# RMSNorm with repeated rows: the first tile by one transfer in place of two halves, gamma in eight pieces in place of seven

## The chip, the cores and the metric

The kernel runs on one core of a Trainium2 chip. The metric is the device time of one execution in microseconds (us), as a median over several executions. The profile's span, from the first to the last instruction, is some 1.8 us shorter than the time: 237.9 us against 239.7 before.

## The reference

```python
# x: (8, 512, 2048) float32, gamma: (2048,) float32
x_rep = np.repeat(x, 2, axis=1)
rms = np.sqrt((x_rep ** 2).mean(axis=-1, keepdims=True) + 1e-6)
return ((x_rep / rms) * gamma[None, None, :]).astype(np.float32)   # (8, 1024, 2048)
```

Each row is normalised, multiplied by gamma and written twice. 33.6 MB come in and 67.1 MB go out.

## The kernel before

The 4096 rows are eight tiles of 128 partitions with four rows each. In the code K = 4 is the rows of a partition and R = 2 the repeats. A tile's buffer holds the 64 KB per partition that go out; x lands in its second half. There are three such buffers, so loads 0, 1 and 2 have free buffers at the start, and each later load waits for a store. All loads and stores are issued by the sync engine, in the order of the program.

```python
def load(i, eng, parts=1):
    y = rows.tile([P, K * R, D], f32, name="y")
    step = K // parts
    for k in range(0, K, step):
        at = K * (R - 1) + k
        eng.dma_start(out=y[:, at : at + step, :], in_=x_t[i, :, k : k + step, :])   # L52
    ys.append(y)
# ... store: nc.sync.dma_start, L56; square: ScalarE, L64 and L68; scale: VectorE, L73 and L74;
# ... repeat: a copy, half on ScalarE and half on VectorE, L81
load(0, nc.sync, parts=2)
gamma_b = singles.tile([P, D], f32, name="gamma_b")
cuts = [0, *range(D // 4, D + 1, D // 8)]            # 512 elements, then six times 256
for c0, c1 in zip(cuts, cuts[1:]):
    nc.scalar.dma_start(out=gamma_b[0:1, c0:c1], in_=gamma[c0:c1].partition_broadcast(1))   # L95
nc.gpsimd.partition_broadcast(out_ap=gamma_b[:], in_ap=gamma_b[0:1, :])                     # L96
# ...
load(1, nc.sync)
load(2, nc.sync)
loads_after = {2: (3, 4, 5), 4: (6, 7)}
for i in range(ntiles):
    compute(i)
    store(i, 0, K)
    for j in loads_after.get(i, ()):
        load(j, nc.sync)
```

The program names no semaphores (counters that a transfer raises when it has landed and for which an engine can wait). The framework gives each transfer one, and this turns out to be what the case is about.

## Time and profile before

| | before |
|---|---|
| time, median of the 5 runs beside the changed kernel | 239.5 us (239.32 to 240.03) |
| span of the profile | 237.9 us |
| VectorE, ScalarE busy | 41%, 42% |
| transfers of the sync queue, share of 16 DMA engines | 98.5% |
| mean rate | 423 GB/s |
| load 1 issued | 8.11 us |
| last packet of load 2 ends | 33.0 us |
| store 0 issued | 27.05 us |

How to read it: only the DMA engines are near full, so what counts is whether their stream has holes. Idle time of the compute engines costs nothing as long as the next store is issued before the engines run dry. Load 2's end and store 0's issue are the pair to compare at the start. The table's last two rows show store 0 six microseconds ahead.

### The profile page before, as it was taken

How to read it: one execution, taken by the hardware profiler on the slowest of the kernel's cores; microseconds unless marked ns; L12 is line 12 of the kernel's file. 1: busy time of each engine (PE TensorE's matmuls, PEld its weight loads, DVE VectorE, ACT ScalarE, POOL GpSimd, SP SyncE). 2: the span in 40 equal slices, each digit the busy share in tenths (PEclk: the TensorE clock that was granted, in tenths of full speed). 3: DMA queues.
4: the chain of work that ended last, by engine and by line, in shares of the span. 5: the costliest groups of instructions: out<-in, count | busy, mean ns of one | idle time of the engine just before them, and what ended most of it. 6: DMA issues, size and time to landing. Idle time of an engine off the chain costs nothing.

```text
span 237.9 us, 287 instructions
## 1 busy us (share of the span) xinstructions
DVE 96.5 (41%) x73; ACT 101.0 (42%) x106; POOL 2.5 (1%) x5
## 2 busy tenths in 40 slices
DVE  0049999960000000059999960000199990000000
ACT  2697999900000000099999920000599960000000
POOL 0030000000000000000000000000000000000000
DMA  7999998989899998999998999989998989999994
GB/s 265 436 446 441 441 441 353 530 353 496 386 452 430 397 485 353 441 441 441 441 518 364 464 419 430 452 369 430 435 518 364 518 364 485 397 452 430 408 474 176
DMA packets 2464, 100.69 MB, mean 423 GB/s; under 512 B 279, under 2 KB 285, under 8 KB 286
## 3 DMA queue, kind: packets, MB, share of 16 engines
q1 hardware_dynamic: 2448, 100.66, 98.5%
q14 instruction: 2, 0.02, 0.0%
q10 hardware_dynamic: 14, 0.01, 0.0%
HBM read 33.56 MB, written 67.11 MB: 423 GB/s over the span
## 4 chain that ended last, share of the span: by engine, by line
DMA 58%; ACT 12%; DVE 9%; issue 1%; POOLq 1%; ACTq 1%; SPq 0%
DMA y<-in_x_dram 33%; DMA out_dram<-y 21%; ACT sq L64 8%; DVE y L74 7%; DMA gamma_b<-in_gamma_dram 4%; ACT y L81 3%; DVE y L81 2%; ACT rms L68 1%; POOLq L136 1%; ACTq L95 1%; DVE rstd L73 0%; POOLq L96 0%; SPq L56 0%
## 5 line engine op out<-in xcount | busy, mean ns | idle before, releaser
L64 ACT ACTIVATE sq<-y 128x2048 f32<-128x2048 f32 x32 | 59.7, 1865 | 87.8 <-DMA y<-in_x_dram 87.8
L74 DVE SCALAR_TENSOR_TENSOR y<-y,rstd,gamma_b 128x2048 f32<-128x2048 f32 x32 | 75.3, 2352 | 4.1 <-POOL gamma_b L96 3.0
L73 DVE RECIPROCAL rstd<-rms 128x1 f32<-128x1 f32 x32 | 5.0, 158 | 94.6 <-ACT rms L68 94.3
L81 ACT COPY y<-y 128x4096 f32<-128x4096 f32 x8 | 28.7, 3590 | 1.4 <-DVE y L74 1.4
L81 DVE COPY y<-y 128x4096 f32<-128x4096 f32 x8 | 18.3, 2294 | 0.3
L68 ACT ACTIVATE rms<-ss,eps_t 128x1 f32<-128x1 f32 x32 | 9.4, 295 | 1.0
L64 ACT ACTIVATION_READ_ACCUMULATOR sq<-y 128x1 f32 x32 | 6.0, 187 | 0.0
L64 ACT ACT_TABLE_LOAD x1 | 1.3, 1283 | 3.0 <-issue 3.0
L96 POOL PARTITION_BROADCAST gamma_b<-gamma_b x1 | 2.3, 2294 | 12.2 <-DMA y<-in_x_dram 12.2
L68 ACT ACT_TABLE_LOAD x1 | 1.3, 1283 | 0.0
L98 DVE MEMSET eps_t<- 128x1 f32 x1 | 0.1, 59 | 0.8 <-PEq L125 0.8
L125 POOL MEMSET const-uint8-127<- 128x1 uint8 x1 | 0.1, 102 | 0.0
L125 POOL MEMSET const-bfloat16-1.0<- 128x1 bf16 x1 | 0.1, 101 | 0.0
L125 POOL MEMSET const-float32-0.0<- 128x1 f32 x1 | 0.1, 98 | 0.2 <-issue 0.2
L125 POOL MEMSET const-float32-1.0<- 128x1 f32 x1 | 0.1, 98 | 0.0
## 6 DMA issues: line engine op xcount, KB each, us to landing
y<-in_x_dram SPq DMA_DIRECT2D x7, 4096.0 KB, 14.6
y<-in_x_dram SPq DMA_DIRECT2D x2, 2048.0 KB, 7.4
out_dram<-y SPq DMA_DIRECT2D x8, 24.4
gamma_b<-in_gamma_dram ACTq DMA_DIRECT2D x6, 1.0 KB
gamma_b<-in_gamma_dram ACTq DMA_DIRECT2D x1, 2.0 KB
```

The source lines that it names most:

```text
L64: nc.scalar.activation(out=sq[:], in_=ys[i][:, K * (R - 1) + k, :], func=Act.Square, accum_out=ss[:])
L68: nc.scalar.activation(out=rms[:], in_=ss[:], func=Act.Sqrt, scale=inv_d, bias=eps_t[:])
L73: nc.vector.reciprocal(out=rstd[:], in_=rms[:])
L74: nc.vector.scalar_tensor_tensor(out=ys[i][:, R * k, :], in0=ys[i][:, K * (R - 1) + k, :], scalar=rstd[:], in1=gamma_b[:], op0=Alu.mult, o ...
L81: copy(out=y_r[:, k0:k1, 1, :], in_=y_r[:, k0:k1, 0, :])
L95: nc.scalar.dma_start(out=gamma_b[0:1, c0:c1], in_=gamma[c0:c1].partition_broadcast(1))
L96: nc.gpsimd.partition_broadcast(out_ap=gamma_b[:], in_ap=gamma_b[0:1, :])
L98: nc.vector.memset(eps_t, eps)
L125: nc = _bacc.Bacc("TRN2", target_bir_lowering=False, num_devices=1)
L136: with _tile.TileContext(nc) as tc:
```

## The change

The intent is fewer and longer transfers: the first tile as one of 4 MB, with 32 KB contiguous per partition and not twice 16 KB, and gamma in eight equal pieces.

```diff
-    load(0, nc.sync, parts=2)
+    load(0, nc.sync)
     gamma_b = singles.tile([P, D], f32, name="gamma_b")
-    cuts = [0, *range(D // 4, D + 1, D // 8)]
+    cuts = [*range(0, D + 1, D // 8)]
     for c0, c1 in zip(cuts, cuts[1:]):
```

## The prediction

> **What bounds the kernel now.** I read the page first: the busy tenths and the queue table.
>
> ```profile
> DVE 96.5 (41%) x73; ACT 101.0 (42%) x106; POOL 2.5 (1%) x5
> ...
> DMA  7999998989899998999998999989998989999994
> ...
> q1 hardware_dynamic: 2448, 100.66, 98.5%
> ```
>
> No compute engine is busy half of the time, while the transfers of the sync queue (q1: all loads of x and all stores) keep the sixteen DMA engines busy for 98.5% of the span. The packet records of the trace (start, length, bytes) say the same more sharply: the first packet of x starts at 1.73 us, the last packet of a store ends at 236.77, and no DMA engine rests for more than 0.34 us anywhere between. A 16 KB packet takes 611 ns, a 32 KB one 1213, a 64 KB one 2418. So the span is a constant sum of bytes plus whatever holes there are in this one stream. **A delay counts if and only if it makes a hole in it.** There are two places at the start where a hole could open, and I looked at both: the issues of loads 0 to 2, and the first store.
>
> The waits of the sync engine, then its timeline from 0 to 2, 2 to 3 and 8.3 to 9 us:
>
> ```profile
> SPq L52 <- DMA y<-in_x_dram: 5.7, 1, 5.7
> ...
> SPq L52 <- DMA gamma_b<-in_gamma_dram: 0.9, 1, 0.9
> ```
>
> ```profile
> 0.72 0.38 SPq L52 DMA_DIRECT2D y<-in_x_dram  x1
> ...
> 2.03 0.33 SPq L52 DMA_DIRECT2D y<-in_x_dram  x1
> ...
> 8.11 0.81 SPq L52 DMA_DIRECT2D y<-in_x_dram  x2
> ```
>
> The source has nothing between the four load issues, and their buffers are free, yet the second half waits 0.9 us for a gamma piece and load 1 waits 5.7 us for the first half of tile 0 to land. The records of the transfers name the semaphores, which explains it. Eight semaphores go round among all transfers in scheduled order, and a transfer that takes a used one waits until its former user has landed. The order is: gamma 1 (first), first half (second), gamma 2 to 7 (third to eighth), second half (first again, hence the wait for gamma 1), load 1 (second again, hence the wait for the first half), load 2 (third again, after gamma 2). Today this costs nothing: when load 1 goes out at 8.11, the second half still has until 12.62 to run on the engines.
>
> The second place, in the timeline from 0 to 32 us:
>
> ```profile
> 8.12 1.88 ACT L64 ACTIVATE sq<-y 128x2048 f32<-128x2048 f32 x1 [3.85 <-DMA y<-in_x_dram]
> ...
> 12.60 2.29 POOL L96 PARTITION_BROADCAST gamma_b<-gamma_b  x1 [12.17 <-DMA y<-in_x_dram]
> ...
> 14.92 2.35 DVE L74 SCALAR_TENSOR_TENSOR y<-y,rstd,gamma_b 128x2048 f32<-128x2048 f32 x1 [3.00 <-POOL gamma_b L96]
> ...
> 27.05 0.35 SPq L56 DMA_DIRECT2D out_dram<-y  x1
> ```
>
> The first scaling waits for gamma (its last piece lands at 12.40 by the chain of waits), and store 0 goes out 12.13 us after it. The DMA engines finish load 2 between 32.41 and 33.00. As an issue needs about 1.0 us to reach the engines (0.72 to 1.73 at the start), store 0 may be as late as 31.4: it has 4.4 us in hand.
>
> **What the Trainium skill says.** "DMA: Bandwidth & Descriptors", section "Queues, rings and completion order": each DMA engine goes round between the queue rows at packet granularity. The trace agrees: gamma's small packets start at 5.65, 6.30, 6.91, 7.56 and so on, one for each 611 ns packet of x. The section "Why a DMA increments its semaphore by 16 and not by 1" says that a copy whose slowest dimension has few elements uses few engines; the trace has 14 packets for 7 gamma transfers (data and semaphore), and the spacing shows all of them queueing behind one engine's packets. The section "Latency and other measured facts" gives about 600 ns to the first byte for transfers issued from sync or scalar; the trace has 1.0 us from the start of the issue to the first packet, and I use that. The section "Rules for kernel authors" asks for at least 1 MiB per DMA; both forms (2 MB, 4 MB) satisfy it, so I expect no gain in rate from the larger one, and the packet times above (2 x 611 against 1213 ns) agree.
>
> **The change part by part.**
>
> *Gamma.* One more issue on the scalar queue, 0.27 us, ahead of an engine that waits for x anyway: nothing. Eight pieces and one load are again nine transfers, so the ring of semaphores comes out the same for all that follows. In scheduled order I expect gamma 1, load 0, gamma 2 to 8, load 1, load 2: the eighth piece takes the first semaphore (free since about 2.0), load 1 takes the second one again, and load 2 the third.
>
> *Load 0 whole.* The bytes, the engines and the stream are those of the two halves, and the second half landed at 13.01; sixteen semaphore packets of 9 ns fewer change nothing, so load 0 lands at about 12.95.
>
> *What moves: load 1's wait.* Its semaphore was that of the first half and is now that of the whole load. It therefore goes out at about 12.96 in place of 8.11, when the engines have run dry, having ended their last packets between about 12.1 and 12.6. The hole can be sized by the same start at the beginning of the kernel: from the issue at 0.72 to the last semaphore packet of the first half at 7.70 are 6.98 us, of which 8 packets x 0.607 = 4.86 us are movement. So a start on empty engines costs 2.12 us. Load 1's last engine then ends at 12.96 + 2.12 + 8 x 1.21 = 24.76, against 22.30 now: **2.5 us later**. A cold first transfer may be slower than this one. With landing 0.4, first byte 1.0 and only some 0.4 us of slow first packets, it would be 1.8. I take 2.2. All of it is on the path that sets the end, since the stream has no slack later in which it could be recovered.
>
> *What moves beside it.* Squares start at 12.97 in place of 8.12. From the first square to the first possible scaling are 3.8 us (8.12 to 11.93, the second table load included), so scaling can start at 16.8, not 14.92. Gamma's pieces meet x packets of twice the length, but only eight of them: in the hole after load 0 the engine is theirs, a piece needs some 0.1 us, and the last should land by 13.8. Broadcast ends by 16.3, before the 16.8. Store 0 goes out at 16.8 + 12.1 = 28.9, 1.9 us later, and load 2 now drains 2.2 us later too: its 4.4 us in hand stay. No second hole.
>
> The sum: 239.7 + 2.2 = **241.9 us**, 0.9% slower.
>
> **The rivals.** *First: load 1 is not held, and gamma starves.* If the scheduled order puts load 1 before gamma 8, load 1 gets the semaphore of gamma 1, goes out at about 2 us, and the stream has no hole at 13. Then each of gamma's packets waits for a 32 KB packet. Five packets of x went before the second piece; with 1.21 us each that puts it at some 8.7 in place of 5.65, and about 12 more turns at 1.24 us end at 23.6. Landing and broadcast put the scaling at 26.5 and store 0 at 38.6, so its packets come at 39.6, 6.8 us after the stream drained: 246.5. If the head start is a time and not five packets, it is about 3 us less: 243.4. For it: the alternation is in the trace. Against it: all gamma pieces preceded the second half in the ring of the kernel before, and load 1 stands where that half stood. *Second: nothing happens*, 239.7: the later tile 0 is hidden by the 4.4 us in hand, and load 1 goes out early for a reason that I don't see. The 5.7 us wait speaks against it. *Third: larger packets are faster.* 611 against 1213/2 ns over 8 packet pairs is below 0.1 us.
>
> **Range and chances.** The hole is 1.8 to 2.5 us by the two ways of sizing, runs of before spread over 0.65 us, and a slow restart or a little of the starved gamma could add one: 241.0 to 243.2. Slower by over 2% means over 244.5, which only the first rival reaches in its worse form: 0.05. Faster has no mechanism: 0.01. Within 2%: 0.94.
>
> **What would show it.** Right: sync waits for x about 11.9 us ahead of load 1, its issue stands near 13.0, few bytes move from 12.6 to 14.5, the first square starts near 13.0, gamma's broadcast starts by 14, store 0 goes out near 29, and the distance from store 0's landing to the end is as now. Wrong: load 1 issued by 3 us or at 8; the scaling waiting for the broadcast until after 20; a hole between load 2 and store 0; or a hole at 13 which the end does not show.

## The result

The changed kernel takes 242.18 us (241.99 to 242.49, five runs), against 239.5 us. The ratio is 1.011, with a 95% interval of 1.0097 to 1.0124. Ratios here are the mean time of one kernel's runs over that of the other's runs in the same rounds, so they aren't quite the ratios of the medians. The change is 1.1% slower: a small loss, clear of noise, and within 2%.

The same parts of the page as before, for the changed kernel (busy time, the DMA row of the slices, the sync queue):

```profile
DVE 96.6 (40%) x73; ACT 101.0 (42%) x106; POOL 2.5 (1%) x5
...
DMA  7979998989898989999999999999999898989894
...
q1 hardware_dynamic: 2304, 100.66, 97.7%
```

The compute engines do what they did. The DMA row has a new 7 in its third slice, which is 12 to 18 us. The waits of the sync engine, and its timeline from 13.2 to 20 us:

```profile
SPq L52 <- DMA y<-in_x_dram: 12.1, 1, 12.1
```

```profile
13.25 0.81 SPq L52 DMA_DIRECT2D y<-in_x_dram  x2
```

The wait of 5.7 us for the first half is now one of 12.1 us for the whole of load 0, and loads 1 and 2 go out from 13.25 us. The wait for a gamma piece is gone, together with the transfer that had it. What this does to the stream is in the table of stretches. Each row gives the stretch, its length, the busy time of VectorE, ScalarE and GpSimd with their instructions, the clock, the mean share of the DMA engines, and GB/s. First before, then changed:

```profile
9.50:12.00 2.50, 0.17 (x1) 2.47 (x5) 0.00 (x0) 1.00 0.98 420
12.00:14.50 2.50, 0.00 (x0) 2.47 (x4) 1.91 (x1) 1.00 0.99 426
14.50:17.00 2.50, 2.08 (x1) 2.47 (x4) 0.39 (x1) 1.00 1.03 446
```

```profile
9.50:12.00 2.50, 0.00 (x0) 0.00 (x0) 0.00 (x0) 1.00 0.97 420
12.00:14.50 2.50, 0.00 (x0) 1.25 (x1) 0.92 (x1) 1.00 0.55 146
14.50:17.00 2.50, 0.10 (x1) 2.47 (x5) 1.38 (x1) 1.00 0.71 275
```

Until 12 us the two are equal at 420 GB/s. Then the changed kernel has 146 GB/s where the kernel before has 426, and 275 GB/s against 446 while the stream restarts. (Rates over short stretches are rough, as a packet's length is of the order of the stretch.) The packet records show the hole engine by engine: the last packets of load 0 end between 11.96 and 12.90 us, and the first ones of load 1 start between 14.21 and 14.68, after 1.3 to 2.7 us. Those sixteen first packets then take 1.71 to 2.12 us in place of 1.21.

Tile 0 in the changed kernel's timeline:

```profile
13.25 1.88 ACT L64 ACTIVATE sq<-y 128x2048 f32<-128x2048 f32 x1 [8.57 <-DMA y<-in_x_dram]
...
13.58 2.29 POOL L96 PARTITION_BROADCAST gamma_b<-gamma_b  x1 [13.16 <-DMA gamma_b<-in_gamma_dram]
...
17.38 2.35 DVE L74 SCALAR_TENSOR_TENSOR y<-y,rstd,gamma_b 128x2048 f32<-128x2048 f32 x1 [0.32 <-DVE rstd L73]
...
29.52 0.35 SPq L56 DMA_DIRECT2D out_dram<-y  x1
```

The first scaling now waits for its own row's statistics and no longer for gamma. Store 0 goes out 2.5 us later than before, but load 2's packets end only at 35.7, so the engines never wait for store 0.

The whole difference can be laid out from the packet records, as means over the sixteen DMA engines, relative to the kernel before. "Idle" is time without a packet of the sync queue, "slow packets" is what packets took beyond 609, 1212 and 2418 ns for 16, 32 and 64 KB (reference values at or 1 to 2 ns below the commonest 611, 1213 and 2418), and "lag" is how far the last engine ends after the mean of the engines:

| us, relative to before | idle | slow packets | lag of the last engine | end of the last packet |
|---|---|---|---|---|
| changed kernel | +2.17 | +0.60 | -0.35 | +2.33 |

The three add up to 2.42. The 0.09 that is missing at the end is rounding, a start that is 0.02 us earlier, and the whole tile's packets, which are 0.05 us shorter in sum (8 x 1212 against 16 x 609 ns). The hole and its restart are the loss.

### The profile page after: what moved, and what is told of

It is laid out like the page before. It is cut to its first block, busy times and chain, and to the rows that moved or that the text cites. A ratio compares the mean times of both kernels' runs of the same rounds, so it can differ in the third digit from the quotient of the medians.

```text
span 240.4 us, 286 instructions
## 1 busy us (share of the span) xinstructions
DVE 96.6 (40%) x73; ACT 101.0 (42%) x106; POOL 2.5 (1%) x5
## 4 chain that ended last, share of the span: by engine, by line
DMA 58%; ACT 13%; DVE 10%; issue 1%; DVEq 0%; SPq 0%
DMA y<-in_x_dram 37%; DMA out_dram<-y 21%; ACT sq L64 8%; DVE y L74 8%; ACT y L81 3%; DVE y L81 2%; ACT rms L68 1%; ACT L68 1%; DVE rstd L73 0%; DVEq L74 0%; SPq L56 0%
## 5 line engine op out<-in xcount | busy, mean ns | idle before, releaser
L96 POOL PARTITION_BROADCAST gamma_b<-gamma_b x1 | 2.3, 2295 | 13.2 <-DMA gamma_b<-in_gamma_dram 13.2
```

## The experiments

The theory is the prediction's: a transfer is held (called the hold below) until the one that had its semaphore eight transfers earlier has landed, and in the changed kernel load 1, the tenth, is held by load 0, the second. The issue records in the traces name the semaphores, and each hold below agrees with them. The main rival is that tile 0 is late as a whole, so that everything after it is. The theory says that the *number* of transfers decides who waits for whom, and numbers are easy to change. All edits are shown against the changed kernel. All results were correct.

### One piece of gamma, load 0 whole: the hold taken away

```diff
-    cuts = [*range(0, D + 1, D // 8)]
+    cuts = [0, D]
```

> Load 0 whole as in the change, gamma in one piece of 8 KB, so that loads 1 and 2 take semaphores nobody has used yet. Theory (the hold of load 1 on load 0's semaphore makes the hole): load 1 goes out by 2 us, no hole at 13 us, first square still at about 13, first scaling at about 17, store 0 at about 29, inside its time in hand: 239.5 us, ratio to before 0.998 to 1.002. Rival (tile 0 coming late as a whole is what the end pays for): as slow as the change, about 242.2, ratio 1.011.

240.29 us (239.68 to 241.37, six runs), ratio 1.0025 (1.0006 to 1.0044). The sync engine's timeline:

```profile
0.72 1.62 SPq L52 DMA_DIRECT2D y<-in_x_dram  x3
29.17 0.35 SPq L56 DMA_DIRECT2D out_dram<-y  x1
```

All three loads are issued by 2.34 us without a wait. The first square still starts at 13.13 and store 0 at 29.17, as late as in the changed kernel, and 2 of the 2.6 us are gone. So the lateness of tile 0 is not what the end pays for. The result is a little above the expected 1.002: 0.6 us remain. In its profile there is no idle time more than before; the last DMA engine lags the mean by 1.57 us, against 0.89.

### Two halves, eight pieces: the hold moved to another place

```diff
-    load(0, nc.sync)
+    load(0, nc.sync, parts=2)
```

> Load 0 in two halves as before, gamma in eight pieces as in the change: ten transfers where both kernels have nine, so the second half now takes the semaphore of the first half. Theory: the second half goes out only at about 8.1, when the engines have run dry at 7.3 to 7.7; the same restart cost as in the change, 2.2 to 2.5 us: 241.7 to 242.1 us, ratio 1.009 to 1.011, with the first square still at 8.1. Rival (tile 0 late as a whole): no loss, 239.5. A rival that blames gamma's late landing: no loss here either, since store 0 has 4.4 us in hand.

242.34 us (four runs), ratio 1.0102 (1.0087 to 1.0117). The sync engine's wait, and the end of its first issues:

```profile
SPq L52 <- DMA y<-in_x_dram: 6.8, 1, 6.8
```

```profile
7.96 1.28 SPq L52 DMA_DIRECT2D y<-in_x_dram  x3
25.10 14.98 SPq L56 DMA_DIRECT2D out_dram<-y  x2
```

(The first line is from the timeline of 8 to 16 us, the second from that of 0 to 40.) With ten transfers the second half is held by the first one. The engines run empty one after the other between 7.18 and 7.60, and their next packets start 1.3 to 2.4 us later. Here load 0 is in halves, its first square is as early as before, gamma arrives earlier than before and store 0 goes out 2 us *earlier* than before, yet the kernel is as slow as the changed one. One gamma piece more, by itself, makes the whole loss. Neither the late tile nor late gamma can explain this; the hold does.

### Seven pieces, load 0 whole: the hold moved to load 2, gamma's packets left in the stream

```diff
-    cuts = [*range(0, D + 1, D // 8)]
+    cuts = [0, *range(D // 4, D + 1, D // 8)]
```

> Load 0 whole, gamma in the seven pieces of before: one transfer fewer, so load 1 takes gamma 1's semaphore and isn't held. Theory: load 1 out at about 2 us, no hole at 13; but now the gamma packets go on alternating with 32 KB packets: last one about 18.5, landing 18.9, broadcast until 21.3, store 0 at about 33.5, its packets at 34.5 after the stream drained at 32.4 to 33.0. A hole of 1.5 to 2.1 us there and slow first packets: about 241.7 us, ratio 1.006 to 1.012, lost at 33 and not at 13. Rival (tile 0 late as a whole): as the change, with store 0 at 29.5 and no hole at 33.

243.33 us (four runs), ratio 1.0152 (1.0138 to 1.0166). Load 1's issue (timeline from 1.5 to 5 us), and the wait of the sync engine for x:

```profile
2.40 0.33 SPq L52 DMA_DIRECT2D y<-in_x_dram  x1
```

```profile
SPq L52 <- DMA y<-in_x_dram: 10.5, 1, 10.5
```

That wait of 10.5 us is load 2's: it has load 0's semaphore and goes out at 13.25, as load 1 does in the changed kernel. It costs nothing, since load 1 is moving until 22.5. Gamma's broadcast and store 0 in the timeline from 0 to 40 us, then the stretch in which the stream has its hole:

```profile
19.45 2.29 POOL L96 PARTITION_BROADCAST gamma_b<-gamma_b  x1 [19.03 <-DMA gamma_b<-in_gamma_dram]
33.91 0.35 SPq L56 DMA_DIRECT2D out_dram<-y  x1
```

```profile
12.00:14.50 2.50, 0.00 (x0) 1.25 (x1) 0.00 (x0) 1.00 0.98 420
...
31.00:35.00 4.00, 3.93 (x4) 3.94 (x7) 0.00 (x0) 1.00 0.62 262
```

The place is as expected: load 1 goes out at 2.40, there is no hole at 13, gamma's packets keep alternating with packets of x (6.50, 7.75, 8.97 and so on to 18.88), and the stream runs dry before store 0 arrives. The size was missed: 3.6 us, not 2.2. Load 2 ended at 31.35 to 32.20, and not at 32.4 to 33.0 as in the kernel before, so the hole is longer: 2.6 to 3.6 us per engine. In the kernel before, 22 packets between 29.1 and 30.9 us are slow, 0.94 us per engine in sum; here slow packets come later, at 90 and 120 us, and there are more of them. I had taken the drain time of one kernel for that of another.

This run also suggests something about the changed kernel: there the hold may not be pure loss. Without it, and with gamma in as many pieces, the start could be slower still; no run has eight pieces and no hold.

### Nine pieces, load 0 whole: the hold given to gamma

```diff
-    cuts = [*range(0, D + 1, D // 8)]
+    cuts = [0, D // 16, *range(D // 8, D + 1, D // 8)]
```

> Load 0 whole, gamma in nine pieces (the first two of 512 bytes): now the ninth gamma piece takes load 0's semaphore, and load 1 takes that of gamma 2, landed by 8. Theory: load 1 out at about 8, no hole at 13; the ninth piece is issued at 13.2 only, and gamma's packets alternate with 32 KB packets until about 22.5; scaling at about 25.4, store 0 at about 37.6, its packets at 38.6, a hole of 5.6 to 6.2 us at 33: about 246 us, ratio 1.024 to 1.030. Rival (only the count of pieces or the whole tile 0 matters, by little): within 0.5 us of the change.

247.05 us (four runs), ratio 1.0304 (1.0291 to 1.0317). The timeline from 12 to 15 us, and that from 0 to 40:

```profile
13.32 0.21 ACTq L95 DMA_DIRECT2D gamma_b<-in_gamma_dram  x1
```

```profile
22.91 2.29 POOL L96 PARTITION_BROADCAST gamma_b<-gamma_b  x1 [22.49 <-DMA gamma_b<-in_gamma_dram]
37.37 0.35 SPq L56 DMA_DIRECT2D out_dram<-y  x1
```

The ninth piece is issued when load 0 has landed, and gamma's last packet follows at 22.2. Store 0 was expected at 37.6 and came at 37.37; the engines rest 5.9 to 6.9 us before its packets. The ratio is just above the expected range, for the same earlier drain (31.4 to 32.3) as with seven pieces.

### Four pieces, with load 0 whole and in halves: is there anything to win?

```diff
-    cuts = [*range(0, D + 1, D // 8)]
+    cuts = [*range(0, D + 1, D // 4)]
```

> Load 0 whole, gamma in four pieces of 2 KB: the hold of load 1 is gone (seven transfers before the ring comes round), and gamma's packets still alternate with 32 KB packets, the last near 12.3, landing at about 12.6 as the fourth piece did in the changed kernel. Theory: no hole at 13 or at 33, store 0 at about 29.3, time as before: ratio 0.998 to 1.004, the upper end if one DMA engine's lag shows again as with one piece. If one 8 KB packet ahead of x on one engine was the reason for the 0.25% of the one-piece kernel, this one is faster than that, near 1.000. Rival (late tile 0): 1.011.

240.26 us (six runs), ratio 1.0026 (1.0011 to 1.0040). The sync engine's timeline from 0 to 40 us:

```profile
0.72 1.33 SPq L52 DMA_DIRECT2D y<-in_x_dram  x3
29.11 0.35 SPq L56 DMA_DIRECT2D out_dram<-y  x1
```

No hold, no hole, and again some 0.6 us more than before. Gamma lands at 12.52 here, nearly as late as in the changed kernel (13.16), so its early landing is not what saved the one-piece kernel. So the guess that one 8 KB packet ahead of x on a single engine was the reason for the 0.25% of the one-piece kernel is not borne out: four pieces of 2 KB cost the same.

The halves with four pieces (the edit above and `parts=2`):

> Load 0 in halves, gamma in four pieces: no hold anywhere on load 0 to 2, gamma lands at about 8 us, first scaling as soon as its square is done, at about 12.0 and not 14.9, store 0 at about 24 to 25. Theory: the stream is full from 1.73 on in this one and in the kernel before, and an earlier store 0 only waits longer in the queue: ratio 0.998 to 1.002. A rival that has the first compute on the path would make it up to 2.5 us faster, ratio 0.99.

239.70 us (five runs), ratio 1.0007 (0.9995 to 1.0019). Its timeline from 12 to 40 us (the first scaling) and from 0 to 40 (the stores):

```profile
12.03 2.35 DVE L74 SCALAR_TENSOR_TENSOR y<-y,rstd,gamma_b 128x2048 f32<-128x2048 f32 x1 [0.16 <-DVE rstd L73]
```

```profile
24.15 13.52 SPq L56 DMA_DIRECT2D out_dram<-y  x2
```

The first scaling comes 2.9 us earlier than before and store 0 as well, and the time stays. The time in hand at store 0 is real in both directions: more of it is worth nothing.

### All of them in one table

The columns are those of the table above, taken relative to the kernel before:

| | idle | slow packets | lag | end of last packet | ratio |
|---|---|---|---|---|---|
| changed (whole, 8 pieces) | +2.17 | +0.60 | -0.35 | +2.33 | 1.011 |
| whole, 1 piece | 0.00 | +0.02 | +0.68 | +0.59 | 1.0025 |
| whole, 4 pieces | +0.02 | +0.18 | +0.11 | +0.26 | 1.0026 |
| halves, 4 pieces | -0.01 | +0.16 | -0.36 | -0.33 | 1.0007 |
| halves, 8 pieces | +1.73 | +0.69 | +0.12 | +2.52 | 1.0102 |
| whole, 7 pieces | +3.19 | +1.12 | -0.27 | +4.00 | 1.0152 |
| whole, 9 pieces | +6.58 | +1.05 | -0.43 | +7.09 | 1.0304 |

The first four columns are of one profiled execution each, the ratio of all timed runs. The kernels without a hold and without a late store have no additional idle time, the others have it at the place that the semaphores and the packets say. None beats the kernel before, in which no DMA engine rests for more than 0.34 us between the first packet and the last.

## Why the prediction was right

*That only holes count.* Right. In the kernel with four pieces and halves store 0 came 2.9 us earlier for nothing; with one piece and the tile whole it came 2.1 us later, and that kernel as a whole cost 0.25% (0.06 to 0.44).

*The ring of semaphores and load 1's wait.* Right, and shown by five counts of pieces: with eight, load 1 is held by load 0; with seven, load 2 is; with nine, a gamma piece is; with one and four, nobody is. The halves with eight pieces moved the hold to the second half.

*Load 0's landing.* 13.25 came in place of 12.96 for load 1's issue. Two DMA engines ended load 0 at 12.77 and 12.90, when the other fourteen were done by 12.35. This may differ from run to run; there is one profile.

*The hole.* The mechanism was right, and the term was sized low: 2.2 us was chosen between 1.8 and 2.5, and the upper way of sizing, the start at the beginning of the kernel, was the better one. By it load 1's last packet was to end at 24.76, and it ended at 24.97, 2.67 us later than before: the issue came 0.29 us late, and the start itself cost 2.0 us (24.97 - 13.25 - 8 x 1.21), against 2.12. (That working took 0.607 us for a 16 KB packet that the prediction itself gives as 611 ns; it changes 2.12 by 0.03.) The end took over 2.33 us of it in the trace, as the last engine lagged less this time. The time rose by 2.68 us between the medians, by 2.41 between the two profiled executions. That 241.9 lies only 0.3 us under the measured 242.18 is in part luck: the sum started from 239.7, and the runs beside the changed kernel had a median of 239.5.

*Tile 0.* Scaling started at 17.38 rather than 16.8, since load 0 landed 0.3 us later and the scaling stood another 0.32 us behind its reciprocal, a wait that the table of waits of the changed kernel lists and the working left out. Gamma's packets did pass in the hole: after six at 1.2 us intervals, the other eight went within 0.2 us, from 12.25 to 12.44. Store 0's time in hand held.

*The rivals.* The first was not what happened, but it describes the seven-piece kernel, with one correction: the head start of x before the second gamma piece is a time and not five packets (6.05 in the changed kernel against 5.65 before, not 8.7). Of the second, the part that a late tile 0 is hidden is shown; that load 1 would go out early is not what happened. On the third, next to nothing was gained by larger packets: 1213 ns is twice 607, against 611.

*What stays open.* Both kernels with a whole first tile and no hold are 0.25% slower than before, and nothing in the start explains it; in the profiles it stands in the lag of the last DMA engine and in slow packets, which fall near 30 us in the kernel before and near 88 and 116 in these. Why they fall there, no run tells. It is about a quarter of what the change cost, so perhaps 2 of the 2.7 us are the hold and the rest belongs to the whole tile, but that split is not shown: the lag of the changed kernel itself was smaller than before.

## What to carry to other kernels

Where a framework hands out a small ring of completion semaphores, a transfer waits for the one that had its semaphore before, so merging, splitting or adding any transfer can shift who waits for whom: count the transfers, and look in the trace for an issue that waits for something that it does not use. On a kernel bound by one stream of transfers, a wait is free while earlier transfers are still moving and costs the whole restart, here over 2 us, once it is for the last one in flight. Small transfers that share a DMA engine with long packets are better few: here each piece of gamma let one 32 KB packet pass before its data and another before its semaphore, 2.5 us in all (6.50, 7.75 and 8.97 us with seven pieces).

## What the Trainium skill lacked or had wrong

- "DMA: Bandwidth & Descriptors" says, under "Rules for kernel authors", to dedicate a semaphore and to prefer few large transfers, and nothing on the time that waiting for a reused semaphore costs a stream. Here that wait decided the result: ratios of 1.011 and 1.0102 where it emptied the DMA engines, against 1.0007 to 1.0026 where none of the first loads was held.
- The same page, "Latency and other measured facts", has about 600 ns to the first byte for sync and scalar transfers, and doesn't say from when it counts. The runs show 1.0 us from the start of the issue to the first packet on empty engines (0.72 to 1.73, and 13.25 to 14.21), which is 0.63 us from the end of the issuing instruction (0.38 and 0.33 us long): counted so, the figure agrees. It has nothing on the packets after that: the first ones took 1.71 to 2.12 us in place of 1.21. With the wait for the landing, a drained stream loses 1.7 to 2.2 us of idle time and 0.7 us of slow first packets per engine.
- The same page, "Queues, rings and completion order", says that a packet drained before switching is typically 9 to 17 descriptors. The trace shows no descriptors, but here a turn was a single packet record, one contiguous run of 16 or 32 KB: gamma's packets stood 0.61 to 0.65 us apart between 16 KB packets and 1.22 to 1.25 us apart between 32 KB packets.
- No page has the slow packets that come once or twice in a run on most engines, 0.9 to 1.9 us per engine in sum, at 29 to 34 us in the kernels with halves and in the changed one, and between 87 and 126 in the other four.
